# Layer 0's sums of squares as two float32r products (a high and a low part) instead of one fp32 product

## The chip, the core and the metric

The kernel runs on one core of a Trainium2 chip. The metric is the device time of one execution in microseconds (us), where lower is better. The core has a matrix engine (PE, with its weight loads listed apart as PEld), a vector engine (DVE), a scalar engine (ACT), a general engine (POOL) and a sync engine (SP) that here only issues DMAs. Each engine executes its own list of instructions in order and waits on semaphores for the others. SBUF is the on-chip memory, PSUM the accumulators that PE writes into and that DVE and ACT can read and write.

## The reference

The reference is a trunk of two layers on a sequence of 1024 positions and a width of 1024. Layer 0 mixes the tokens by differential attention, layer 1 by forgetting attention, and each is followed by a gated MLP with a short convolution. What the change touches is the norm behind the values of layer 0, over the 128 components of each of 8 heads:

```python
def rms_norm(x, g):
    xf = x.astype(jnp.float32)
    y = xf * lax.rsqrt(jnp.mean(xf * xf, -1, keepdims=True) + RMS_EPS) * g.astype(jnp.float32)
    return y.astype(x.dtype)
...
        s = jnp.einsum('bhcqd,bhckd->bhcqk', qb, k) * scale
        p = masked_softmax(s, causal_mask(start, Q_BLOCK, S))
        a = (p[:, :, 0] - lam * p[:, :, 1]).astype(v.dtype)
        o = jnp.einsum('bhqk,bhkd->bqhd', a, v)
        o = rms_norm(o, subln_g) * (1.0 - lambda_init)
```

and, in layer 1, the running sum of the forget gates, `c = jnp.cumsum(log_f, axis=1)`.

## The kernel before

**Products.** The inputs and the weights are fp32. A large product isn't done as one fp32 product but as three products in float32r, a shorter format that PE takes at a higher rate: `split` (lines 87 and 89) makes a high part by a copy on ACT and a low part by a subtraction on DVE, and `mm3` (lines 98 to 100) issues high by high, high by low and low by high into one accumulator. Nearly all lines of PE in the profile are therefore L98, L99 and L100.

**Layer 0's attention** takes about 60 to 540 us of the span. It runs over eight pairs of attention maps (one head of values each), some 57 us apiece. For each pair the loop in `attention` interleaves two streams by hand. One is the filler: 48 steps of `project`, the projection of the next pair's queries, keys and values (for the last pair: the output projection). The other is the pair's jobs. `diff_scores` makes one block of 128 queries against 128 to 1024 keys: PE products (L506, L507), a masked minimum on DVE (L509, into a small column `nm`), the exponential on ACT (L531), and normalising on DVE (L534 to L541). `Values` takes 256 queries at a time: it transposes the weights of the maps on PE by the identity (L1337), splits them into `pt` tiles (L87, L89), and multiplies them with the values (`m<-pt,q` at L98 to L100) into the left 256 columns of a PSUM bank, `ob`.

**The norm.** When such a value block is complete, `diff_values` runs, four times per pair and 32 times in all. In the layout here the 128 components of a head lie on the partitions, so the sum of squares runs over partitions. It copies the block out of PSUM (L553, ACT, `of<-m`), squares it (L556, ACT, into the left half of a 512-wide tile `sq`), and after two turns of the loop hands one fp32 product to a queue that the next turn empties: a matrix of ones by the squares (L562, PE, `m<-sq,ones`), 128x256, into the right half of the same bank `ob`. Every partition then holds the sum. ACT makes the reciprocal root by Ln and Exp (L567, L568, into the right half of `sq`) and its square (L569), and DVE multiplies (L571) and applies a correction step (L572, L573). The bank is free after L572.

**Buffers.** PSUM holds four banks of kind `m` (projections, transposes, values, norms) and two double banks of kind `s` (scores). The `wst` tiles, two of them, serve the staging of weights by DMA (L107) and also the second map's exponentials. Rotary steps move pieces of the projected tiles by DMA (L264, L454 to L469) and transpose them on PE (L475).

**Order.** The code above issues instructions in the order of the Python loop; the framework's scheduler then decides the order within each engine's list and the banks. A changed instruction can therefore move its neighbours too.

**Layer 1's gates.** `gate_logits` creates a constant tile `tri` and loads it (L592, L593). `forget_gates` forms the gates in a 1024-wide tile `w`, whose last 128 columns it leaves unused, and uses `ones` as an operand of a running sum. `forget_sums` multiplies by `tri` (L630).

Of the kernel before, what the change touches and what calls it, by code (L numbers as in the profile page):

```python
# [9 lines left out]
F32 = mybir.dt.float32  # L10
F32R = mybir.dt.float32r
BF16 = mybir.dt.bfloat16
I32 = mybir.dt.int32
AF = mybir.ActivationFunctionType
ALU = mybir.AluOpType
# [4 lines left out]
P = 128  # L20
# [34 lines left out]
class Trunk:  # L55
# [64 lines left out]
    def consts(self):  # L120
        nc, cp, i = self.nc, self.cp, self.i
        self.ident = cp.tile([P, P], F32, name="ident")
        nc.sync.dma_start(self.ident, i["ident"])
        mask = self.spare()[:, :P]
        nc.sync.dma_start(mask, i["mask"])

        self.mask = cp.tile([P, S], BF16, name="mask")
        nc.gpsimd.memset(self.mask[:, :S - P], 0.0)
        nc.vector.tensor_scalar(self.mask[:, S - P:], mask, -1.0, None, op0=ALU.mult)

        self.qz = [[cp.tile([P, P], F32R, name=f"qz{h}{b}") for b in range(2)] for h in range(2)]
        for h in range(2):
            for t in self.qz[h]:
                nc.gpsimd.memset(t[64 - 64 * h:128 - 64 * h, :].bitcast(F32), 0.0)
        self.nz = [0, 0]
        self.ones = cp.tile([P, P], F32, name="ones")
        nc.vector.memset(self.ones, 1.0)
        self.cw, self.cb = [], []
        for l in range(2):
            cw = cp.tile([P, NF, 3], F32, name=f"cw{l}")  # L140
            cb = cp.tile([P, NF], F32, name=f"cb{l}")
            nc.sync.dma_start(cw, i["cw"][l])
            nc.sync.dma_start(cb, i["cb"][l])
            self.cw.append(cw)
            self.cb.append(cb)
        self.eps_rms = cp.tile([P, 1], F32, name="eps_rms")
        nc.vector.memset(self.eps_rms, RMS_EPS)
        self.eps_ln = cp.tile([P, 1], F32, name="eps_ln")
        nc.vector.memset(self.eps_ln, LN_EPS)
        self.gsub = cp.tile([P, 1], F32, name="gsub")  # L150
        nc.sync.dma_start(self.gsub, i["subln"])
        nc.vector.tensor_scalar(self.gsub, self.gsub, (1.0 - LAM_INIT) * -0.5 / P, None, op0=ALU.mult)
# [397 lines left out]
    def diff_values(self, of, ob, c4):  # L550
        nc = self.nc
        osl = of[:, c4 * 256:c4 * 256 + 256]
        nc.scalar.copy(osl, ob[:, :256])  # L553
        sr = self.tp.tile([P, 512], F32, tag="sq", name=self.nm("sq"), bufs=1)
        sq, rd = sr[:, :256], sr[:, 256:]
        nc.scalar.activation(sq, osl, AF.Square)  # L556
        for _ in range(FL):
            yield

        ms, done = ob[:, 256:], []  # L560
        yield
        self.after(1, lambda: done.append(nc.tensor.matmul(ms, self.ones, sq, start=True, stop=True)))  # L562
        yield
        while not done:
            yield

        nc.scalar.activation(rd, ms, AF.Ln, scale=1.0 / P, bias=self.eps_rms)  # L567
        nc.scalar.activation(rd, rd, AF.Exp, scale=-0.5)  # L568
        nc.scalar.activation(sq, rd, AF.Square)  # L569
        yield  # L570
        nc.vector.scalar_tensor_tensor(osl, osl, self.gsub, rd, op0=ALU.mult, op1=ALU.mult)  # L571
        nc.vector.scalar_tensor_tensor(sq, ms, P * RMS_EPS, sq, op0=ALU.add, op1=ALU.mult)  # L572
        nc.vector.scalar_tensor_tensor(osl, sq, -3.0 * P, osl, op0=ALU.add, op1=ALU.mult)  # L573
# [4 lines left out]
    def gate_logits(self, c):  # L578
        nc = self.nc
        if c == 0:  # L580
            st = self.tmp()[:, :P]
            nc.sync.dma_start(st, self.i["wf"])
            w = self.tmp(F32R, pool=self.pp, tag="p")
            self.wf = w[:, :P], w[:, P:2 * P]
            for t in self.qz[0] + self.qz[1]:
                nc.gpsimd.memset(t[64:66, :].bitcast(F32), 1.0)
            self.split(*self.wf, st)
            self.bf = self.cp.tile([16, 1], F32, name="bf")
            nc.sync.dma_start(self.bf, self.i["bf"])
            self.z = self.tmp()  # L590
            self.zd = self.dr.tile([16, 1024], F32, name="zd")
            self.tri = self.cp.tile([P, P], F32, name="tri")  # L592
            nc.sync.dma_start(self.tri, self.i["tri"])  # L593
        ps = self.mbank()
        for kt in range(KT):
            ws = slice(16 * kt, 16 * kt + 16)
            self.mm3(ps[:16], self.wf[0][:, ws], self.wf[1][:, ws], self.xh[kt, c], self.xl[kt, c],
                     kt == 0, kt == KT - 1)
        nc.vector.tensor_scalar(self.z[:16, c * 512:c * 512 + 512], ps[:16], self.bf, None, op0=ALU.add)

    def forget_gates(self):

        nc = self.nc
        nc.sync.dma_start(self.zd, self.z[:16])
        w = self.tmp(pool=self.pp, tag="p")
        z, e, u, l, c = [w[:, j * P:j * P + P] for j in range(5)]
        self.chl = w[:, 5 * P:7 * P].bitcast(F32R)

        nc.sync.dma_start(z, self.zd.rearrange("h (b t) -> (h b) t", t=P))

        nc.vector.scalar_tensor_tensor(u, z, -1.0, z, op0=ALU.mult, op1=ALU.max)
        nc.scalar.activation(e, u, AF.Exp, scale=-1.0)
        nc.vector.tensor_scalar(u, e, 2.0, None, op0=ALU.add)
        nc.vector.reciprocal(u, u)
        nc.vector.tensor_tensor(e, e, u, op=ALU.mult)
        nc.vector.tensor_tensor(u, e, e, op=ALU.mult)
        nc.vector.tensor_scalar(l, u, 1.0 / 17, None, op0=ALU.mult)
        for k in (15, 13, 11, 9, 7, 5, 3, 1):
            nc.vector.scalar_tensor_tensor(l, l, 1.0 / k, u if k > 1 else e, op0=ALU.add, op1=ALU.mult)
        nc.vector.tensor_scalar(z, z, 0.0, None, op0=ALU.min)  # L620
        nc.vector.scalar_tensor_tensor(l, l, -2.0, z, op0=ALU.mult, op1=ALU.add)
        nc.vector.tensor_tensor_scan(c, self.ones, l, 0.0, op0=ALU.mult, op1=ALU.add)
        self.c = c

    def forget_sums(self, t):
# [924 lines left out]
```

## Time and profile before

| | |
|---|---|
| median of three runs | 2452.82 us (2452.7 to 2454.08) |
| span of the profiled execution | 2450.4 us |
| what lies around the span (median less span) | 2.4 us |
| PE / DVE / ACT busy, share of the span | 98% / 78% / 51% |
| share of the chain of waits: PE / DVE / DMA / ACT | 79% / 9% / 5% / 4% |

The page gives no second time for the profiled execution itself; its span and the 2.4 us around it stand for it. The profile was read on the span's own clock, with 0 at its first instruction. A row of the timeline begins with the start and the duration of one instruction; in square brackets stands the idle time of the engine ahead of it and what ended it. The durations of PE's instructions overlap, since the products are pipelined: what a product costs is the distance from its start to the next start, not its duration. On DVE and ACT too, one row's end can lie some 0.08 us behind the next one's start.

### The profile page before, as it was taken

Reading aid. Unit: us, or ns where it says so; the run is one execution under the profiler, and the core shown is the slowest. Engines: PE = TensorE matmul, PEld = TensorE weight load, DVE = VectorE, ACT = ScalarE, POOL = GpSimd, SP = SyncE. Lnnn points to the kernel's source line nnn. Section 1 sums busy time; section 2 is a strip of 40 time slices with the busy share of each in tenths; the row PEclk is TensorE's granted clock in tenths of the full one; section 3 lists DMA queues with packets and bytes.
Section 4 is the critical chain, followed back from the end, with each engine's and each line's share of the span. In section 5 each row is a group of like instructions: output and inputs, shape, how many; then the busy total and the mean of one; then the engine's idle time right before and its main releaser. Section 6 shows DMA issues by size and latency. Waiting matters only on the chain.

```text
span 2450.4 us, 33602 instructions
## 1 busy us (share of the span) xinstructions
PE 2411.6 (98%) x11803; PEld 2012.9 (82%) x11803; DVE 1908.4 (78%) x3731; ACT 1259.5 (51%) x2388; POOL 141.6 (6%) x321
## 2 busy tenths in 40 slices
PE   8999999999999999999999999999999999999998
PEld 6888888888888888888778888888888888888886
DVE  5777777989866677887867777778898676678977
ACT  4565666646544444544545555556465444445444
POOL 2101111110000000000101000000010000000000
PEclk9999999999999999999999999999999999999999
DMA  5232223622222223975232222224223222228751
GB/s 175 72 84 82 76 77 91 219 80 93 89 92 78 78 78 132 349 231 162 104 82 66 65 65 66 66 74 164 78 95 103 78 78 90 91 99 323 263 169 69
DMA packets 116033, 283.39 MB, mean 116 GB/s; under 512 B 18108, under 2 KB 25276, under 8 KB 115864
## 3 DMA queue, kind: packets, MB, share of 16 engines
q1 hardware_dynamic: 115064, 279.34, 35.5%
q8 instruction: 93, 1.52, 0.3%
q0 software_dynamic: 800, 1.90, 0.2%
q14 instruction: 76, 0.62, 0.1%
HBM read 188.44 MB, written 59.18 MB: 101 GB/s over the span
## 4 chain that ended last, share of the span: by engine, by line
PE 79%; DVE 9%; DMA 5%; ACT 4%; issue 2%; SPq 1%; POOL 0%; DVEq 0%; ACTq 0%; POOLq 0%
PE m L98 19%; PE m L100 19%; PE m L99 19%; PE s L98 3%; PE s L99 3%; PE s L100 3%; PE m L1337 3%; PE s L507 2%; PE s L506 2%; DMA wst<-in_w 1%; DMA pt<-in_wd 1%; PE m L1363 1%; PE m L1362 1%; DVE s L509 1%; DVE wo L89 1%
## 5 line engine op out<-in xcount | busy, mean ns | idle before, releaser
L98 PE MATMUL m<-xh,wh 128*128 128x512 f32 x768 | 322.8, 420 | 9.3 <-ACT xh L87 8.8
L100 PE MATMUL m<-xh,wl 128*128 128x512 f32 x768 | 304.3, 396 | 0.5 <-DVE wl L89 0.5
L99 PE MATMUL m<-xl,wh 128*128 128x512 f32 x768 | 302.1, 393 | 0.7 <-DVE xl L89 0.7
L98 PE MATMUL m<-xh,wo 128*128 128x512 f32 x656 | 255.5, 389 | 0.9 <-DVE xl L89 0.9
L99 PE MATMUL m<-xl,wo 128*128 128x512 f32 x656 | 255.2, 389 | 0.0
L100 PE MATMUL m<-xh,wo 128*128 128x512 f32 x656 | 255.2, 389 | 0.0
L509 DVE CUSTOM_DVE_ANT_0 s<-s,mask 128x128 f32<-128x128 f32 (+7 forms) x256 | 194.2, 759 | 48.2 <-PE s L507 47.5
L87 ACT ACTIVATE wo<-wg 128x512 fp32r<-128x512 f32 x168 | 106.2, 633 | 224.8 <-PE m L100 215.8
L87 ACT ACTIVATE pt<-m 128x512 fp32r<-128x512 f32 (+1 forms) x240 | 128.2, 552 | 127.6 <-PE m L1337 92.6
L98 PE MATMUL m<-q,wo 128*128 128x512 f32 x472 | 184.0, 390 | 0.0
L99 PE MATMUL m<-q,wo 128*128 128x512 f32 x472 | 183.6, 389 | 0.0
L100 PE MATMUL m<-q,wo 128*128 128x512 f32 x472 | 183.6, 389 | 0.0
L98 PEld LDWEIGHTS m<-xh,wh 128*128 128x128 f32 x768 | 145.7, 190 | 33.1 <-ACT xh L87 8.8
L100 PEld LDWEIGHTS m<-xh,wl 128*128 128x128 f32 x768 | 144.9, 189 | 33.1 <-DVE wl L89 1.5
L99 PEld LDWEIGHTS m<-xl,wh 128*128 128x128 f32 x768 | 146.0, 190 | 23.4 <-DVE xl L89 1.2
L89 DVE TENSOR_TENSOR pt<-m,pt 128x512 fp32r<-128x512 f32 (+1 forms) x240 | 148.6, 632 | 20.9 <-ACT pt L87 17.8
L87 ACT ACTIVATE wo<-t 128x512 fp32r<-128x512 f32 x132 | 82.8, 627 | 140.7 <-PE m L100 133.3
L501 POOL CAST qz<-q 64x128 fp32r<-64x128 f32 x256 | 97.7, 383 | 864.7 <-PE s L507 825.0
L89 DVE TENSOR_TENSOR wo<-wg,wo 128x512 fp32r<-128x512 f32 x168 | 115.2, 687 | 39.9 <-ACT wo L87 39.1
L98 PEld LDWEIGHTS m<-xh,wo 128*128 128x128 f32 x656 | 123.1, 188 | 27.2 <-PE m L929 1.4
L100 PEld LDWEIGHTS m<-xh,wo 128*128 128x128 f32 x656 | 123.2, 188 | 25.7
L99 PEld LDWEIGHTS m<-xl,wo 128*128 128x128 f32 x656 | 123.1, 188 | 25.3
(333 smaller groups left out, 6022.0 us busy)
## 6 DMA issues: line engine op xcount, KB each, us to landing
wst<-in_w SPq DMA_DIRECT2D x46, 512.0 KB
t<-in_wi SPq DMA_DIRECT2D x44, 512.0 KB
ha<-ad SPq DMA_DIRECT2D x88, 256.0 KB
wg<-in_wi SPq DMA_DIRECT2D x42, 512.0 KB
ad<-t SPq DMA_DIRECT2D x42, 512.0 KB
q<-q SPq DMA_DIRECT2D x128, 128.0 KB
pt<-in_wd SPq DMA_DIRECT2D x24, 512.0 KB
hb<-in_wd SPq DMA_DIRECT2D x44, 256.0 KB
```

The costliest lines, as they stand in the source:

```text
L87: nc.scalar.activation(hi, src, AF.Copy, scale=1.0 if scale is None else scale)
L89: nc.vector.tensor_tensor(lo, src, hi.bitcast(F32), op=ALU.subtract)
L98: mm(out, wh, xh, start=start, stop=False)
L99: mm(out, wh, xl, start=False, stop=False)
L100: mm(out, wl, xh, start=False, stop=stop)
L501: nc.gpsimd.tensor_copy(qz[r:r + 64, :], q[r:r + 64, qt * P:qt * P + P])
L506: nc.tensor.matmul(sb[:, ks], q[:, qt * P:qt * P + P], kd[:, ks], start=True, stop=False)
L507: nc.tensor.matmul(sb[:, ks], qz[rows], kl[rows, ks], start=False, stop=True)
L509: nc.vector.tensor_tensor_reduce(sb[:, :ln], sb[:, :ln], self.mask[:, S - ln:], 1.0, BIG, ALU.add, ALU.min, mn)
L1337: nc.tensor.transpose(tb[:, w:w + P], self.pts[q][:, kt * P:kt * P + P], k.ident)
L1362: mm(o, self.v[0][:, vs], h, start=first, stop=False)
L1363: mm(o, self.v[0][:, vs], l, start=False, stop=last)
```

## The change

The squares now go through PSUM and are split. ACT writes them into the right half of the bank (`ms`), copies them from there in float32r (`hi`), and DVE subtracts that from the squares (`lo`). PE then does two float32r products with a float32r matrix of ones, accumulated into `ms`, in place of the one fp32 product. The reciprocal root goes into the left half of the bank, its square into a new small tile `sr`. `tri` is no longer a tile of its own; it is loaded into the unused columns of `w` in `forget_gates`.

```diff
-        self.ones = cp.tile([P, P], F32, name="ones")
-        nc.vector.memset(self.ones, 1.0)
+        self.ones = cp.tile([P, P], F32R, name="ones")
+        nc.vector.memset(self.ones.bitcast(F32), 1.0)
...
         nc.scalar.copy(osl, ob[:, :256])
-        sr = self.tp.tile([P, 512], F32, tag="sq", name=self.nm("sq"), bufs=1)
-        sq, rd = sr[:, :256], sr[:, 256:]
-        nc.scalar.activation(sq, osl, AF.Square)
+        sr = self.tp.tile([P, 512], F32R, tag="sq", name=self.nm("sq"), bufs=1)
+        hi, lo = sr[:, :256], sr[:, 256:]
+        ms, done = ob[:, 256:], []
+        nc.scalar.activation(ms, osl, AF.Square)
+        nc.scalar.copy(hi, ms)
+        nc.vector.tensor_tensor(lo, ms, hi.bitcast(F32), op=ALU.subtract)
...
-        self.after(1, lambda: done.append(nc.tensor.matmul(ms, self.ones, sq, start=True, stop=True)))
+        def sums():
+            nc.tensor.matmul(ms, self.ones, hi, start=True, stop=False)
+            nc.tensor.matmul(ms, self.ones, lo, start=False, stop=True)
+            done.append(True)
+
+        self.after(1, sums)
...
+        sq, rd = self.tp.tile([P, 256], F32, tag="sr", name=self.nm("sr"), bufs=1), ob[:, :256]
...
-            self.tri = self.cp.tile([P, P], F32, name="tri")
-            nc.sync.dma_start(self.tri, self.i["tri"])
...
         self.chl = w[:, 5 * P:7 * P].bitcast(F32R)
+        self.tri = w[:, 7 * P:]
+        nc.sync.dma_start(self.tri, self.i["tri"])
...
-        nc.vector.tensor_tensor_scan(c, self.ones, l, 0.0, op0=ALU.mult, op1=ALU.add)
+        nc.vector.tensor_tensor_scan(c, self.ones.bitcast(F32), l, 0.0, op0=ALU.mult, op1=ALU.add)
```

In the changed program the lines of the norm are: Square L557, the copy to `hi` L558, the subtraction L559, the two products L566 and L567, then L576 to L578 on ACT and L580 to L582 on DVE (before: L567 to L569 and L571 to L573). The list of PE grows by 32 instructions, that of DVE by 32 instructions (30 rows, since some stand grouped), that of ACT by 32.

The order moves at many places. The first one shown is in pair 2, where the product follows soonest after its squares. PE's list there before (the names end in the number of the buffer; `m_1370` is the bank of the norm, `s_1523` a score bank):

```order
L100 MATMUL m_1507<-xh_250,wl_1140 128x512
L506 MATMUL s_1523<-q_564,q_562 128x512
L562 MATMUL m_1370<-sq_1385,ones 128x256
L507 MATMUL s_1523<-q_565,qz_300 128x512
L506 MATMUL s_1523<-q_564,q_562 128x256
L507 MATMUL s_1523<-q_565,qz_300 128x256
L98 MATMUL m_1531<-pt_1482,q_566 128x256
```

And PE's list now at the same place (`m_1384` is the bank of the norm, `s_1543` the scores, `m_1551` the values), from the fourth value product on; ahead of these rows stand the four score products and three value products:

```order
L98 MATMUL m_1551<-pt_1501,q_566 128x256
L99 MATMUL m_1551<-pt_1501,q_566 128x256
L100 MATMUL m_1551<-pt_1501,q_567 128x256
L98 MATMUL m_1527<-xh_256,wh_1147 128x512
L99 MATMUL m_1527<-xl_257,wh_1147 128x512
L100 MATMUL m_1527<-xh_256,wl_1148 128x512
L98 MATMUL m_1527<-xh_260,wh_1147 128x512
L566 MATMUL m_1384<-sq_1399,ones 128x256
L567 MATMUL m_1384<-sq_1399,ones 128x256
L99 MATMUL m_1527<-xl_261,wh_1147 128x512
```

The pair of products stands behind the four score products, six value products and four filler products, where the one product stood behind the first score product. DVE's list at the same place before:

```order
L534 RECIPROCAL rs_1587<-ls_1481 128x1
L536 TENSOR_SCALAR p_1545<-p_1545,rs_1587 128x768
L509 ISA s_1523,nm_1528<-s_1523,mask 128x768
L509 ISA nm_1528 128x1
L571 SCALAR_TENSOR_TENSOR of_1377<-of_1377,gsub,sq_1385 128x256
L572 SCALAR_TENSOR_TENSOR sq_1385<-m_1370,sq_1385 128x256
L573 SCALAR_TENSOR_TENSOR of_1377<-sq_1385,of_1377 128x256
L534 RECIPROCAL rs_1635<-ls_1530 128x1
```

And DVE's list there now:

```order
L534 RECIPROCAL rs_1607<-ls_1500 128x1
L536 TENSOR_SCALAR p_1565<-p_1565,rs_1607 128x768
L509 ISA s_1543,nm_1548<-s_1543,mask 128x768
L509 ISA nm_1548 128x1
L559 TENSOR_TENSOR sq_1399<-m_1384,sq_1399 128x256
L534 RECIPROCAL rs_1657<-ls_1550 128x1
L540 TENSOR_TENSOR rs_1657<-rs_1657,nlam 128x1
L541 SCALAR_TENSOR_TENSOR p_1565<-wst_1610,rs_1657,p_1565 128x768
L580 SCALAR_TENSOR_TENSOR of_1391<-of_1391,gsub,m_1384 128x256
L581 SCALAR_TENSOR_TENSOR sr_1517<-m_1384,sr_1517 128x256
```

The new subtraction (L559) stands right behind the minimum of the scores, and the norm's own last steps moved behind the normalising of the next map. The second place is on DVE in pair 3, ahead of the transposes of the rotary step. Before:

```order
L534 RECIPROCAL rs_2325<-ls_2235 128x1
L536 TENSOR_SCALAR p_2294<-p_2294,rs_2325 128x896
L89 TENSOR_TENSOR wl_2341<-wst_2256,wh_2340 128x1024
L509 ISA s_2282,nm_2287<-s_2282,mask 128x896
L509 ISA nm_2287 128x1
L89 TENSOR_TENSOR pt_2322<-m_2296,pt_2322 128x512
```

And now:

```order
L89 TENSOR_TENSOR wl_2380<-wst_2294,wh_2379 128x1024
L559 TENSOR_TENSOR sq_2284<-m_2222,sq_2284 128x256
L534 RECIPROCAL rs_2363<-ls_2271 128x1
L536 TENSOR_SCALAR p_2332<-p_2332,rs_2363 128x896
L509 ISA s_2320,nm_2325<-s_2320,mask 128x896
L509 ISA nm_2325 128x1
L89 TENSOR_TENSOR pt_2360<-m_2334,pt_2360 128x512
```

The low part of a weight slab (`wl`) moved ahead of the normalising of the first map (L534, L536), and the new subtraction stands between them. On SP, the load of that slab (L107, `wst_2256` before, `wst_2294` now) moved ahead of one DMA of the rotary step. SP's list in layer 1 takes the load of `tri` (L616) between the stores that end layer 0: five of them stand ahead of it, one and two weight loads behind it.

More of the change, by code (lines that the diff above doesn't have):

```diff
@@ L553, in diff_values @@
         nc.scalar.copy(osl, ob[:, :256])
-        sr = self.tp.tile([P, 512], F32, tag="sq", name=self.nm("sq"), bufs=1)
-        sq, rd = sr[:, :256], sr[:, 256:]
-        nc.scalar.activation(sq, osl, AF.Square)
+        sr = self.tp.tile([P, 512], F32R, tag="sq", name=self.nm("sq"), bufs=1)
[4 more added lines that the diff above has]
+        nc.vector.tensor_tensor(lo, ms, hi.bitcast(F32), op=ALU.subtract)
         for _ in range(FL):
             yield
-        ms, done = ob[:, 256:], []
         yield
-        self.after(1, lambda: done.append(nc.tensor.matmul(ms, self.ones, sq, start=True, stop=True)))
+        def sums():
[3 more added lines that the diff above has]
+        self.after(1, sums)
         yield
```

## Prediction

> **What bounds the kernel now.** I read the page's busy line and its chain of waits first, then busy time by windows of layer 0's attention, then the lines of the norm one by one.
>
> ```profile
> PE 2411.6 (98%) x11803; PEld 2012.9 (82%) x11803; DVE 1908.4 (78%) x3731; ACT 1259.5 (51%) x2388; POOL 141.6 (6%) x321
> PE 79%; DVE 9%; DMA 5%; ACT 4%; issue 2%; SPq 1%; POOL 0%; DVEq 0%; ACTq 0%; POOLq 0%
> 120.00:180.00 60.00, 59.61 (x321) 50.56 (x320) 47.26 (x113) 36.35 (x80) 5.48 (x17) 1.00 0.30 84
> 420.00:480.00 60.00, 57.77 (x310) 48.77 (x309) 54.84 (x127) 38.65 (x82) 7.95 (x15) 1.00 0.66 210
> 480.00:540.00 60.00, 59.40 (x302) 49.57 (x301) 52.28 (x105) 30.51 (x60) 3.73 (x8) 1.00 0.26 88
> sum 480.00, PE 468.30 PEld 397.37 DVE 390.10 ACT 287.89 POOL 53.07; mean PE 58.54 PEld 49.67 DVE 48.76 ACT 35.99 POOL 6.63
> ```
>
> The window rows give busy us of PE, PEld, DVE, ACT and POOL, then the granted clock of PE (1.00 in each); the sum is over the eight windows from 60 to 540. PE sets the end: it is busy for 98% and holds 79% of the chain. In the stretch that the change touches it stands still for only 0.4 to 2.2 us of each 60. DVE is the next one: 79% busy in the middle pairs (47.26 of 60), 91% and 87% in the last 120 us. So a microsecond of PE's own time is worth about a microsecond, if what feeds PE is ready earlier too, and added time on DVE is free in the middle and dear at the end. ACT has room everywhere.
>
> **What the norm's product costs PE.** The line's own view, two stretches of PE's timeline, and the place where the product waits:
>
> ```profile
> L562 PEld LDWEIGHTS m<-sq,ones x64: 186/188/192, 69.5 to 529.2; 128*128 128x128 f32 x64
> ...
>   ACT sq L556: 6.2, 13
> ```
>
> ```profile
> 90.24 0.39 PE L100 MATMUL m<-xh,wl 128*128 128x512 f32 x1
> 90.47 0.59 PE L562 MATMUL m<-sq,ones 128*128 128x256 f32 x2
> 90.71 0.59 PE L98 MATMUL m<-xh,wh 128*128 128x512 f32 x1
> 91.14 0.40 PE L99 MATMUL m<-xl,wh 128*128 128x512 f32 x1
> ...
> 133.58 0.28 PE L98 MATMUL m<-pt,q 128*128 128x256 f32 x1
> 133.70 0.28 PE L99 MATMUL m<-pt,q 128*128 128x256 f32 x1
> ```
>
> The 32 fp32 products appear as 64 records, two for each. From L100's start at 90.24 to L99's at 91.14 are 0.90 us, in which two 128x512 products of 0.23 (90.24 to 90.47) and the fp32 product run: 0.90 − 0.46 = **0.44 us** for it. A float32r product of the same 128x256 shape is 0.12 from start to start (133.58, 133.70), each with weights of its own; over longer rows of them (eight from 133.35 to 134.30 in that stretch) it is 0.117. The new pair is thus 0.235 us, and 0.44 − 0.235 = 0.205 us saved, 32 times: **−6.5 us**. This is the surest term. Its bounds: none saved, if float32r with `ones` were no cheaper (a rival below), and 6.5.
>
> **The wait ahead of it.** PE waits for the squares (L556) 13 times, records of PE and PEld together. Six products stand right behind their squares, the first of the four norms in each of pairs 2 to 7, at 132.58, 189.32, 247.13, 304.32, 362.32 and 419.31; the first and the last:
>
> ```profile
> 131.92 0.39 PE L506 MATMUL s<-q,q 128*128 128x512 f32 x1
> 132.58 0.70 PE L562 MATMUL m<-sq,ones 128*128 128x256 f32 x2 [0.27 <-ACT sq L556]
> 133.35 0.28 PE L506 MATMUL s<-q,q 128*128 128x256 f32 x1
> 133.47 0.28 PE L507 MATMUL s<-q,qz 128*128 128x256 f32 x1
> ...
> 419.31 0.70 PE L562 MATMUL m<-sq,ones 128*128 128x256 f32 x2 [0.27 <-ACT sq L556]
> ```
>
> From L506 to the next L506 are 1.43 us. Two 128x512 products and the fp32 one need 0.46 + 0.44 = 0.90, so 0.53 is lost at each, 3.2 in all. The other 26 products come late enough behind their squares that PE loses little there: the whole 6.2 us of that wait are mostly the same six counted on both PE and PEld.
>
> In the changed order the pair stands behind four score products, six value products and four filler products. PE reaches it at 131.92 + 2 × 0.23 + 8 × 0.117 + 4 × 0.23 = 134.24. Is `lo` ready then? On ACT and DVE stand:
>
> ```profile
> 132.10 0.42 ACT L556 ACTIVATE sq<-of 128x256 f32<-128x256 f32 x1
> ```
>
> ```profile
> 133.78 0.96 DVE L509 CUSTOM_DVE_ANT_0 s<-s,mask 128x768 f32<-128x768 f32 x1 [1.47 <-PE s L507]
> 134.67 0.14 DVE L509 DVE_READ_ACCUMULATOR2_ANT nm<- 128x1 f32 x1
> 134.67 0.48 DVE L571 SCALAR_TENSOR_TENSOR of<-of,gsub,sq 128x256 f32<-128x256 f32 x1
> ```
>
> The square ends at 132.5 there, and with the copy behind it `hi` is there at about 132.9; where the scheduler now puts one more 0.6 us evacuation ahead of it, at 133.5 at the latest. On DVE the subtraction comes behind the minimum (L509), which began 0.31 after the last score product had begun (133.47 to 133.78) and held DVE 0.89. That score product now begins at 131.92 + 0.46 + 0.117 = 132.50, the minimum at 132.81, the subtraction at 133.70, and it ends by 134.12, a tenth ahead of PE. So the wait goes, and the next thing late is nothing near: I take **−3.2 us**. The margin is a tenth; if the subtraction comes late the loss of 0.53 may stay, so the bounds are 0 and −3.2.
>
> **What is added on DVE and ACT.** No such copy or subtraction of 128x256 is in the trace; the nearest rows:
>
> ```profile
> L571 DVE SCALAR_TENSOR_TENSOR of<-of,gsub,sq 128x256 f32<-128x256 f32 x32 | 15.4, 481 | 2.5 <-ACT sq L568 2.0
> L572 DVE SCALAR_TENSOR_TENSOR sq<-m,sq 128x256 f32<-128x256 f32 x32 | 13.4, 419 | 0.7 <-ACT sq L569 0.7
> L553 ACT COPY of<-m 128x256 f32<-128x256 f32 x32 | 11.7, 367 | 23.9 <-PE m L100 23.9
> L89 DVE TENSOR_TENSOR pt<-m,pt 128x384 fp32r<-128x384 f32 x31 | 17.1, 553 | 1.8 <-ACT pt L87 1.1
> ```
>
> The copy out of PSUM is 0.37 us (L553), the subtraction 0.42 (L572, which reads PSUM and SBUF at the same size; the split of 128x384 at 0.553 bounds it from above). That is 32 × 0.37 = 11.8 us on ACT and 32 × 0.42 = 13.4 us on DVE. The other steps of the norm keep their number and size and only change between PSUM and SBUF; rows of either kind lie between 0.37 and 0.48, so I count them at 0, with ±0.07 each at most, on ACT and DVE where they are covered by idle time. On ACT the cover is 40% idle time. On DVE in pairs 1 to 6 it is 21% of idle time, some 12 us per pair against 4 × 0.42 = 1.7 us. Two places have no such cover.
>
> *The rotary transposes (L475).* Their wait is the largest of PE's in this stretch:
>
> ```profile
> PEld m L475 <- DVE pt L89: 8.5, 5, 2.2
> ```
>
> ```profile
> 203.49 1.15 DVE L541 SCALAR_TENSOR_TENSOR p<-wst,rs,p 128x896 f32<-128x896 f32 x1
> ...
> 209.95 1.22 DVE L89 TENSOR_TENSOR wl<-wst,wh 128x1024 fp32r<-128x1024 f32 x1 [1.03 <-ACT wh L87]
> ...
> 212.24 0.55 DVE L89 TENSOR_TENSOR pt<-m,pt 128x384 fp32r<-128x384 f32 x1
> ...
> 212.84 0.65 PE L475 MATMUL m<-ident,t 128*128 128x128 f32 x4 [1.57 <-DVE pt L89]
> ```
>
> In five pairs a chain ends here: L541 frees a `wst` tile, a weight slab is loaded into it, ACT and DVE split it (`wl` at 209.95), then minimum, `pt`, and the bank that L475 needs. One new subtraction now lies on DVE ahead of L541 in the same chain, behind the earlier `wl`. That is +0.42 per pair, 5 × 0.42 = 2.1 if nothing offsets it. The slab before it is loaded earlier now, ahead of a DMA of the rotary step; that can give back a part of the 1.03 us that DVE waited for `wh`. I take half of the added cost, **+1 us**, with bounds of −2.5 (half of the 1.03 gained in five pairs) and +5 (as much as that wait lost in five).
>
> *The last pair and the tail (420 to 540 us).* With DVE at 91% and 87%, PE's savings there are largely set by DVE. A quarter of the 32 products stands in these 120 of 480 us: 8 × 0.20 = 1.6 us of gain may not be collected, and 8 × 0.42 = 3.4 us are added to DVE. Bounds 0 and +5.0; I take **+2 us**, the lower half, because PE too was still 96 to 99% busy there (57.77 and 59.40 of 60).
>
> **The move of `tri`.** Before, its load stood early, and now it stands among the stores that end layer 0:
>
> ```profile
> L593 SPq DMA_DIRECT2D tri<-in_tri x1: 423/423/423, 51.0 to 51.0; - x1
> 1185.54 21.46 SPq L1482 DMA_DIRECT2D hd<-acc  x5
> ```
>
> SP spends 0.42 us on it. The stores around it take 21 us of SP's time while PE works on in layer 1, which hides it. I count 0; without that cover it would delay the weight loads behind it by 0.4, and longer only if it had to wait for its tile.
>
> **Sum.** −6.5 − 3.2 + 1 + 2 = −6.7 us. Against the profiled execution's span of 2450.4 and the 2.4 us around it, 2452.8, that is **2446 us**; the median of the runs shown is 2452.82, the same. The best ends (−6.5, −3.2, −2.5, 0) give 2440.6, the worst that keeps the saving (−6.5, 0, +5, +5) gives 2456.3.
>
> **Rivals.**
>
> *The gain is absorbed.* PE arrives 0.2 us earlier at every later wait, and if that wait is set by DVE (L475, banks freed by L89, the tail), it only gets longer. For it: DVE has got more work, not less, and 8.5 us of PEld's wait are at L475. Against it: in all of 60 to 540 us PE idles for 480 − 468.3 = 11.7 us, so DVE binds at few points. If only a quarter of the 9.7 remains, 2450.4. Chance 0.28.
>
> *The weights bind, and the pair is no cheaper.* The load of `ones` shows 188 ns, and the pair has two, 0.38 us, against 0.44: then 32 × 0.06 = 2 us are saved, 2450.8. Against it: the value products with a load each run at 0.12 in the rows above, so these loads lie beside the products. 0.07. The Trainium skill (Perfetto Trace Analysis, Identifying the Most-Contended Engine) says that PE's headroom is read from the busy share of the weight loads rather than from that of the products. The number of loads, 64, stays the same here, so by that rule alone nothing would be saved, 2452.8; the spacing of 0.12 at 188 ns a load speaks against it.
>
> *Slower: DVE is stopped in front of the minimum.* DVE runs in order. Where the subtraction stands ahead of a minimum (L509) and `hi` isn't there yet, DVE waits for square and copy, and 0.37 + 0.42 = 0.79 us pass before the minimum, the exponential behind it, and PE's next transposes and banks. If this reaches PE at 24 of 32 places, 24 × 0.79 = 19.0 us stand against 9.7: +9.3, 2462. It turns slower from 12 to 13 places. For it: PE waits on `pt` and on banks freed by DVE in the rows above. Against it: at both places shown the subtraction stands behind a minimum or a `wl`, when ACT has long copied. 0.10.
>
> **How the numbers follow.** Forecast 0.55, absorbed 0.28, weights 0.07, slower 0.10. The measurement of this kernel can tell about 0.2%, 4.9 us, from no change: faster means below 2447.9, slower above 2457.7. That gives 0.55 faster, 0.35 within, 0.10 slower. The range is 2440 to 2456: from the best ends of the terms to the worst, with the two middle rivals inside and the slower one left out.
>
> **What would show it.** Of the saving: L566 and L567 0.12 apart on PE, and PE's busy time in 60 to 540 us shorter by 6 us. Of the wait: no idle time at the six pairs, or one that now names DVE (`sq` at L559). Of DVE: 13.4 us more busy time, the subtraction at 0.42, without a new entry at L509. At L475 waits within half a microsecond of those before. It is wrong if a new wait of PE on DVE shows in most pairs, if the pair stands 0.4 apart, or if layer 1, where only `tri` changes, moves by over 1 us.

## The result, and the profile after

The changed kernel takes 2467.24 us in the median of five runs (2461.55 to 2471.29), against 2452.82 before: a ratio of 1.0059 with an interval of 1.0048 to 1.007. It is slower by 0.6%, beyond the range of the prediction. The profiled execution is the fastest of the five (2461.55 us, span 2459.8). The spread of 10 us is wide beside the 1.4 us of the five runs before, but in the later runs of this case the kernel before spread over 5.0 to 7.4 us too (21 to 28 runs each).

The page's busy line and chain of waits of the changed kernel:

```profile
PE 2410.2 (98%) x11803; PEld 2013.4 (82%) x11803; DVE 1919.4 (78%) x3763; ACT 1264.6 (51%) x2420; POOL 138.3 (6%) x321
PE 75%; DVE 10%; DMA 6%; ACT 4%; SPq 2%; issue 2%; DVEq 0%; POOL 0%; ACTq 0%
```

PE has lost four points of the chain, to DVE, DMA and SP's queue above all. Three windows of layer 0's attention (PE, PEld, DVE, ACT, POOL, then the granted clock), behind the first one as it was before:

```profile
180.00:240.00 60.00, 58.16 (x316) 49.60 (x315) 46.12 (x114) 37.11 (x82) 7.00 (x16) 1.00 0.28 76
...
180.00:240.00 60.00, 56.77 (x307) 48.59 (x307) 46.46 (x113) 36.18 (x82) 5.90 (x16) 0.97 0.27 76
300.00:360.00 60.00, 57.15 (x317) 48.92 (x316) 48.20 (x118) 37.20 (x84) 6.65 (x17) 1.00 0.28 76
420.00:480.00 60.00, 56.59 (x296) 47.58 (x296) 53.31 (x126) 38.27 (x85) 5.06 (x14) 0.97 0.66 211
```

And PE's wait at the rotary transposes from the view of waits, first as it was before, then the two lines of the changed kernel:

```profile
PE m L475 <- DVE pt L89: 6.3, 5, 1.8
...
PEld m L475 <- DVE pt L89: 16.4, 5, 3.6
PE m L475 <- DVE pt L89: 14.2, 5, 3.2
```

Two things stand there. PE's wait at L475, five times in pairs 3 to 7 as before, has grown from 6.3 to 14.2 us on PE. And the granted clock, 1.00 in every one of the eight windows before, is 0.97 in four of the eight now.

From the first score product to the first product of the MLP's weights, PE needed 519.5 us before (48.5 to 568.0) and 529.5 now (47.6 to 577.1). That is 10.0 us more, against 9.4 for the whole span: what lies ahead of this stretch and behind it is 0.6 us shorter. Within that stretch the pair itself does what it was meant to:

```profile
203.56 0.28 PE L566 MATMUL m<-sq,ones 128*128 128x256 f32 x1
203.68 0.28 PE L567 MATMUL m<-sq,ones 128*128 128x256 f32 x1
203.79 0.40 PE L98 MATMUL m<-xh,wh 128*128 128x512 f32 x1
```

The two products take 0.23 us in place of 0.44. In the groups by form, the added instructions cost what was estimated, and DVE hardly stops for the copy:

```profile
L559 DVE TENSOR_TENSOR sq<-m,sq 128x256 fp32r<-128x256 f32 x32 | 13.4, 419 | 0.5 <-ACT sq L558 0.5
L558 ACT CAST sq<-m 128x256 fp32r<-128x256 f32 x32 | 11.9, 371 | 0.8
L557 ACT ACTIVATE m<-of 128x256 f32<-128x256 f32 x32 | 12.4, 387 | 0.7
L577 ACT ACTIVATE m<-m 128x256 f32<-128x256 f32 x32 | 11.9, 372 | 0.5
```

Where does the wait at L475 come from? Here is the chain in pair 3, SP's queue first. Before (the first `wst` load, and the second, which is the one that L475 waits for in the end):

```profile
192.69 0.53 SPq L264 DMA_DIRECT2D q<-q  x1
193.26 0.58 SPq L107 DMA_DIRECT2D wst<-in_w  x1
193.94 1.55 SPq L264 DMA_DIRECT2D q<-t  x2
...
202.95 1.22 SPq L456 DMA_DIRECT2D t<-t  x2
204.27 1.33 SPq L107 DMA_DIRECT2D wst<-in_w  x1
```

And after, with DVE's and PE's rows of the same chain in a fence of their own behind them:

```profile
191.25 0.59 SPq L107 DMA_DIRECT2D wst<-in_w  x1
191.99 0.50 SPq L264 DMA_DIRECT2D q<-q  x1
...
193.89 0.53 SPq L264 DMA_DIRECT2D q<-q  x1
196.60 0.46 SPq L264 DMA_DIRECT2D q<-t  x1
...
203.55 1.84 SPq L456 DMA_DIRECT2D t<-t  x2
205.50 0.53 SPq L107 DMA_DIRECT2D wst<-in_w  x1
```

```profile
203.06 1.15 DVE L541 SCALAR_TENSOR_TENSOR p<-wst,rs,p 128x896 f32<-128x896 f32 x1
...
210.37 1.23 DVE L89 TENSOR_TENSOR wl<-wst,wh 128x1024 fp32r<-128x1024 f32 x1 [1.30 <-ACT wh L87]
...
213.26 1.11 PE L475 MATMUL m<-ident,t 128*128 128x128 f32 x4 [2.94 <-DVE pt L89]
```

Before, the first load (512 KB) was issued right behind the small move q<-q at 192.69. Now it is issued ahead of it. SP then stands from 194.4 to 196.6, and the view of SP's waits (188 to 210 us) says for what:

```profile
SPq L264 <- DMA q<-q: 2.1, 1, 2.1
```

It is the move q<-q that was issued at 191.99, some 4.6 us earlier. Before, a move that waited for the q<-q of 192.69 could go by 195.0, 2.3 us later. The semaphore events of the traces show the same in all of pairs 3 to 7: from its issue to its landing this move takes 4.5 to 4.9 us in the changed kernel, and 2.3 to 3.2 before. All rotary moves behind are late by that, and with them the second load. It is issued at 205.50 although L541 had freed its tile by 204.2; before, it was SP that stood ready at 204.27 and L541 that came last (204.6).

The same in the five pairs, each value taken from such rows (end of L541 to the end of the load's issue; start of L475 less the end of the product before it at 0.23 us):

| | pair 3 | pair 4 | pair 5 | pair 6 | pair 7 | sum |
|---|---|---|---|---|---|---|
| L541 to load issued, before | 0.96 | 0.30 | 0.16 | 0.66 | 0.31 | 2.4 |
| L541 to load issued, after | 1.81 | 1.43 | 1.05 | 2.35 | 0.05 | 6.7 |
| PE's loss at L475, before | 1.73 | 1.12 | 1.93 | 0.92 | 1.43 | 7.1 |
| PE's loss at L475, after | 3.10 | 3.38 | 2.95 | 3.34 | 2.28 | 15.1 |

In pair 7 the load is no longer late, and the loss still grows by 0.85 us, so the load's place is not all of it.

The lower clock lies right behind these losses. Two-microsecond windows around the first of them:

```profile
208.00:210.00 2.00, 2.00 (x11) 1.65 (x11) 1.04 (x3) 0.72 (x1) 0.00 (x0) 1.00 0.31 115
210.00:212.00 2.00, 0.32 (x2) 0.00 (x0) 1.63 (x2) 1.89 (x5) 0.00 (x0) 1.00 0.19 49
212.00:214.00 2.00, 0.73 (x4) 0.74 (x5) 2.00 (x6) 1.17 (x3) 0.00 (x0) 0.70 0.29 66
214.00:216.00 2.00, 2.00 (x7) 1.61 (x6) 1.79 (x5) 1.04 (x3) 0.00 (x0) 0.50 0.13 30
216.00:218.00 2.00, 2.00 (x14) 1.83 (x13) 1.28 (x5) 1.02 (x3) 0.29 (x1) 0.95 0.90 206
```

PE has nothing to do from about 210.3 to 213.3. The lost shares of the clock (0.30 + 0.50 + 0.05 of two us each, 1.7 us) are those of half clock for 3.4 us, from about 212.8 on. There are four such stretches, at 96, 212, 390 and 451 us (the first behind two waits of 1.4 and 1.1 us close together, the others behind L475), and none in the profile of before, apart from the last few us of the span, where both kernels are at half clock. PE's products in each take about 1.5 us longer than outside, 6 us together. Over the runs, the mean granted clock falls with the time (0.996 at 2461.55 and 2463.02 us, 0.995 at 2467.24, 0.993 and 0.994 at 2470.44 and 2471.29). One stretch takes 0.0007 off that mean (1.7 of some 2465 us), so the two slowest runs, at 0.002 and 0.003 less than the fastest, hold an estimated three to four stretches more. At about 1.5 us each that is some 4 to 6 of the 9 to 10 us between them; the rest of the spread isn't explained.

The account of the 10.0 us: −6.5 for the pairs, −3.2 for the six waits (none of PE's waits names the squares now), +7.9 at L475, +6 of half clock, and +3.3 of other waits of PE, nearly all on DVE (idle times above 0.1 us in PE's rows: 7.4 us, against 4.1 before, without L475 and L562). That is 7.5 in all. About 2.5 us are left, in waits too short for the view to list.

### The profile page after: what moved, and what is told of

Same layout as the page of the kernel before. It is cut to its first block, busy times and chain, and to the rows that moved or that the text cites. A ratio compares the mean times of both kernels' runs of the same rounds, so it can differ in the third digit from the quotient of the medians.

```text
span 2459.8 us, 33674 instructions
## 1 busy us (share of the span) xinstructions
PE 2410.2 (98%) x11803; PEld 2013.4 (82%) x11803; DVE 1919.4 (78%) x3763; ACT 1264.6 (51%) x2420; POOL 138.3 (6%) x321
## 4 chain that ended last, share of the span: by engine, by line
PE 75%; DVE 10%; DMA 6%; ACT 4%; SPq 2%; issue 2%; DVEq 0%; POOL 0%; ACTq 0%
PE m L98 19%; PE m L100 18%; PE m L99 18%; PE s L98 3%; PE s L100 3%; PE s L99 3%; PE m L1346 3%; DMA wst<-in_w 2%; PE s L507 2%; PE s L506 2%; PE m L1372 1%; DVE s L509 1%; PE m L1371 1%; DMA pt<-in_wd 1%; DVE wo L89 1%
## 5 line engine op out<-in xcount | busy, mean ns | idle before, releaser
L98 PE MATMUL m<-xh,wh 128*128 128x512 f32 x768 | 319.6, 416 | 10.3 <-ACT xh L87 9.5
```

What stands on the lines that cost most here:

```text
L98: mm(out, wh, xh, start=start, stop=False)
```

## The experiments

The theory after the result, **S**: the slab load's new place on SP makes L475 late, and the long waits lower the clock on top of that. The first rival, **D**: the added subtraction on DVE makes L475 late. Each kernel is compared with the kernel before as it was measured beside it: that median was 2449.66 or 2450.57 us here, where it had been 2452.82.

**The change with the loads held back, and the kernel before with the loads ahead.** A helper adds an issue order on SP, for the first load of each of pairs 3 to 7, and nothing else:

```diff
+LOADS = (186, 234, 282, 330, 378)
+LATE_LOADS = ((0, -6), (0, 3), (-5, 0))
+EARLY_LOADS = ((0, -7), (-6, 0), (2, 0))
+def pin(tc, edges):
...
+    for k in LOADS:
+        for later, earlier in edges:
+            tc.add_manual_dep(own[k + later], own[k + earlier].name,
...
+            if l == 0:
+                pin(self.tc, LATE_LOADS)
```

Here `own` is the list of SP's DMAs in the order of the code. The second kernel is the one before with `EARLY_LOADS`; its PE instructions keep their order.

> The change, with one thing held as before: in pairs 3 to 7 SP issues the weight slab's load (L107 of before) behind the first q<-q move and the four rotary moves that it stood behind before, and ahead of the next. Theory S (the load's place on SP made the transposes of L475 late: from the end of L541 to the load's issue 1.34 us on average in the changed kernel, 0.48 before): that distance falls to about 0.5 us, PE's waits at L475 fall from 15.0 us to 10 or 11, the half-clock stretches behind them become fewer, and the time falls to 2452 to 2458 us. Theory D (the added subtraction on DVE made them late): the waits stay at 14 to 15 us and the time at 2461 to 2471.

> The kernel before, with one thing taken from the change: in pairs 3 to 7 SP issues the weight slab's load ahead of the first q<-q move. Nothing on PE is changed. Theory S: the waits at L475 grow from 7.1 us to 11 or 12, and the time to 2456 to 2462 us (some half-clock stretches among it). Theory D: waits of 7 us and 2452 to 2454 us.

The change with the loads held back took 2452.34 us, 1.0005 of the kernel before (0.9996 to 1.0014): the whole slowdown is gone. The kernel before with the loads ahead took 2460.26, 1.0038 (1.0025 to 1.0052): most of the slowdown appears without any change on PE. PE's waits of the two kernels, the first with the loads behind:

```profile
PE m L491 <- DVE pt L105: 8.7, 5, 2.3
```

```profile
PE m L491 <- DVE pt L105: 10.1, 5, 2.6
```

(L491 is L475 of the other kernels; the helper moves the lines.) From the end of L541 to the load's issue are now −0.7 to 0.8 us with the loads behind, and 0.8 to 1.7 in the first four pairs with the loads ahead. By the measure of the table, PE's loss at L475 is 9.5 us with the loads behind and 10.9 with the loads ahead, each a little less than S had said. The move q<-q lands 2.3 to 2.5 us after its issue in the first kernel, as before, and 4.4 to 5.0 us in the second, as in the changed one. The first profile has no stretch of half clock, the second has two. S stands, from both sides, and so does the step in it that the move lands late behind the load. It doesn't account for all: the restored kernel should have been faster than before by the 9.7 us that PE saves, and is level.

**The high part alone, and the fp32 product with the added work.** The first leaves out the low part of the squares, so DVE gets nothing more; the second keeps the fp32 product and adds the copy and the subtraction. Both have the loads ahead.

```diff
-        nc.vector.tensor_tensor(lo, ms, hi.bitcast(F32), op=ALU.subtract)
...
-            nc.tensor.matmul(ms, self.ones, hi, start=True, stop=False)
-            nc.tensor.matmul(ms, self.ones, lo, start=False, stop=True)
+            nc.tensor.matmul(ms, self.ones, hi, start=True, stop=True)
```

```diff
+        nc.scalar.activation(s32, osl, AF.Square)
+        nc.scalar.copy(hi, s32)
+        nc.vector.tensor_tensor(spare, s32, hi.bitcast(F32), op=ALU.subtract)
...
+            nc.tensor.matmul(ms, self.ones.bitcast(F32), s32, start=True, stop=True)
```

> The change without the low part: no subtraction on DVE, and one float32r product (the squares rounded to float32r) where the change has two. SP issues the loads ahead of the q<-q moves, as in the change. PE does 32 x 0.117 = 3.7 us less than in the change, DVE 13.4 us less. Theory D: waits at L475 back at 7 to 8 us and a time of 2441 to 2447 us. Theory S: waits at L475 of 11 us or more, and 2452 to 2462 us.

> The kernel with the fp32 product, but with the change's copy on ACT and subtraction on DVE added (their results aren't used) and the change's other tiles. PE does what it did before, DVE 13.4 us more. SP issues the loads ahead of the first q<-q move, behind one of the moves. Theory D: waits at L475 of 10 to 13 us and 2456 to 2464 us. If DVE's added work is free and only the load's place counts: waits of 9 to 12 us by the load alone, and the distance from the end of L541 to the load's issue above 0.9 us; if that distance is at 0.5 and the waits still grow, it is DVE.

The high part alone took 2451.33 us, level with before (1.0, 0.9992 to 1.0009), and PE's waits at L475 were 11.8 us: S was right about the waits there, and the time lies 0.7 us below its range. The fp32 product with the split took 2464.68, 1.0056 (1.0043 to 1.0068), with 12.6 us at L475, three stretches of half clock, and 1.6 us from L541 to the load in three of five pairs. It is 4.4 us above the kernel with the loads ahead and nothing added. So D may have a part too, a smaller one; this kernel has one stretch of half clock more than that one, and its squares lie in SBUF.

**The same with the loads held back, and the subtraction moved or doubled.** Two new names for what absorbs PE's saving once the loads are back: **D2**, the added subtraction; **A**, PE only arrives earlier at waits that DVE sets. The four kernels: the low part made on POOL from squares in SBUF (the diff), the high part alone, the fp32 product with the split, and the change with the subtraction written twice; all four with `LATE_LOADS`.

```diff
+        nc.scalar.activation(sq, osl, AF.Square)
+        nc.scalar.copy(hi, sq)
+        nc.gpsimd.tensor_tensor(lo, sq, hi.bitcast(F32), op=ALU.subtract)
```

> The change with the loads held behind the q<-q move as before, and with the low part made on POOL (from squares that ACT leaves in SBUF) in place of DVE. PE does the same as in the change. Theory D2 (with the loads back in their place, the added subtraction on DVE, ahead of L541, is what absorbs PE's saving of 9.7 us): waits at L475 of 6 to 8 us, and 5 to 9 us faster than the kernel before on the same chip. Theory A (PE only arrives earlier at waits that DVE sets anyway, whatever is added): within 2 us of the kernel before.

> One float32r product of the high part, no subtraction, the loads behind the q<-q move as before. PE does 32 x (0.44 - 0.117) = 10.3 us less than before and has no wait of 3.2 us for a product at once behind its squares if it is moved as in the change. Theory D2: 8 to 13 us faster than the kernel before, waits at L475 of 6 to 8 us. Theory A: 1 to 5 us faster, waits at L475 of 10 us or more. Against the same kernel with the loads ahead (2451.3): theory S says 4 us or more faster.

> The fp32 product kept, copy and subtraction added (results unused), the loads behind the q<-q move as before: only ACT's and DVE's added work is left of the change. Theory D2: 5 to 9 us slower than the kernel before, waits at L475 above 9 us. Theory A: within 2 us of it. Against the same kernel with the loads ahead (14.1 us above the kernel before on that chip): theory S says at least 6 us less.

> The change with the loads behind the q<-q move as before, and the subtraction done twice: DVE gets another 13.4 us of work. Theory D2: 4 to 9 us slower than the same kernel with one subtraction (which was 1.8 us above the kernel before), waits at L475 2 us or more above its 9.5. Theory A: within 2 us of it.

| kernel, loads held back | median us (before 2449.66) | ratio, interval | PE's wait at L475 |
|---|---|---|---|
| low part on POOL | 2447.04 | 0.999 (0.9982 to 0.9999) | 1.8 |
| high part alone | 2445.71 | 0.998 (0.9971 to 0.9989) | 7.7 |
| fp32 product with split | 2457.05 | 1.003 (1.0018 to 1.0042) | 8.9 |
| subtraction twice | 2453.06 | 1.0012 (1.0003 to 1.0021) | 8.4 |

S holds again in size, taking each kernel against the one before that was measured beside it: the high part alone is 3.9 us faster than before with the loads back, where it was 0.8 slower, and the fp32 product with the split loses 7.4 where it lost 14.1. Between D2 and A the runs are divided. The doubled subtraction adds 32 rows of 0.42 us on DVE (8.2 us of busy time, 1918.8 to 1927.0) and some 1.6 us to the time (3.4 above before, where one subtraction was 1.8 above), which is A's; two stretches of half clock are in its profile, and none in that of one subtraction. The split on an fp32 product costs 7.4, which is D2's; but there DVE stopped for ACT's copy:

```profile
DVE sr L576 <- ACT sq L575: 3.9, 8, 0.6
```

That is 3.9 us, against 0.5 in the change, and one stretch of half clock is in its profile, so its price is not that of the work alone. And the low part on POOL took L475's wait almost away, from 8.7 to 1.8 us. It was 2.6 us faster than before, so 4.4 us better than the same with the subtraction on DVE (1.8 above before). That lies between the theories, D2 with 5 us or more faster than before and A within 2. The products now waited for POOL:

```profile
PE m L584 <- POOL sq L576: 2.3, 8, 0.6
PE m L491 <- DVE pt L105: 1.8, 4, 0.6
```

**Nothing added at all, the tile alone, POOL with more time, and the change again.** In the first, ACT writes the squares in float32r and one product sums them (the low part is left out); the loads are held back. The second is the kernel before with only `tri` moved. The third is the kernel with POOL and one more `yield` ahead of the products.

```diff
+        nc.scalar.activation(hi, osl, AF.Square)
...
+            nc.tensor.matmul(ms, self.ones, hi, start=True, stop=True)
```

```diff
-        for _ in range(FL):
+        for _ in range(FL + 1):
```

> ACT writes the squares rounded to float32r, and one float32r product sums them: no copy, no subtraction, nothing added on DVE or ACT (the low part is left out). The loads stand behind the q<-q move as before. PE does 32 x (0.44 - 0.117) = 10.3 us less than before. Theory A (what PE saves is mostly waited for again at DVE's later points, whatever is added): 2 to 6 us faster than the kernel before. Theory D2 (the added copy and subtraction took the gain): 9 to 13 us faster.

> The kernel before with only the load of tri moved into layer 1, to the unused columns of w. If the move is free, as forecast: within 1 us of the kernel before, and waits at L475 of 7 us in layer 0 as before. If the move holds the weight loads behind it: over 2 us slower.

> The low part on POOL, the loads behind the q<-q move, and the pair of products one turn of the loop later. In the run without the later turn PE waited 2.3 us for POOL's low part and 1.1 us for ACT's high part. If those waits are worth their time: gone, and 1 to 3 us faster than that run (which was 2.6 us faster than the kernel before), so 3.5 to 5.5 us faster than before. Theory A (PE only waits elsewhere): within 1 us of that run.

> The change as it is, on the chip of the other runs of this call. 8 to 18 us slower than the kernel before, with three to nine stretches of half clock, each behind a wait of PE at L475 or at a bank freed by DVE.

With nothing added the kernel took 2443.78 us against 2450.57, 0.9971 (0.9959 to 0.9982): 6.8 us faster, of 10.3 that PE no longer does. That lies between the two theories. PE waits 9.5 us at L475 there, 3 more than before. So about a third of what PE saves is waited for again, though DVE and ACT do no more than before. `tri` alone: 2450.13, 0.9998 (0.9989 to 1.0006), no difference. POOL with one more turn: 2446.47, 0.9981 (0.9972 to 0.999), 4.1 us faster than before; the waits that it was to remove are still there (2.0 us for POOL, 1.1 for ACT), so its mechanism was wrong, and its gain over the kernel without the turn lies within the intervals. Of the kernels that keep both parts of the squares it is the fastest, and faster than both kernels of this case. The change again: 2462.59 us against 2450.57, 1.0054 (1.0041 to 1.0067), with four stretches of half clock, two of them nearly 7 us long.

## Why the prediction was wrong

- **What a product costs: right.** 0.23 us for the pair in place of 0.44, −6.5 us. The rival that the weight loads bind is out: each of the pair's two loads still shows 188 ns.
- **The wait for the squares: right.** None of PE's waits is left there; the weight loads wait 1.1 us in six places for the subtraction, at most 0.2 at a time.
- **The added instructions: right.** 0.419 and 0.371 us against 0.42 and 0.37. DVE's busy time grew by 11.0 us, not by the 13.4 of the sum, which fits neighbouring rows that overlap by some 0.08 us each.
- **The rotary transposes: this step failed.** "The slab before it is loaded earlier now, ahead of a DMA of the rotary step; that can give back a part of the 1.03 us that DVE waited for `wh`." The moved load was seen and given the wrong sign. It was counted for itself and not for what stands behind it in SP's queue: a small move whose landing the next rotary moves wait for. They, and the second load behind them, became late. The term was +1 us with bounds of −2.5 and +5; it measured +7.9. The loads held back take 5.6 of that away (15.1 to 9.5 by the table's measure). The prediction's own sign, waits at L475 within half a microsecond of those before, failed in each of the five pairs (+0.85 to +2.42).
- **A consequence that was no term: the clock.** With waits of up to 3.4 us at L475, the granted clock halves behind some of them. That is 6 us in the profiled run, and by the estimate above a part of the spread of the others.
- **The last pair and the tail: too dear, as far as the last pair goes.** From the seventh pair's store (477.9 before, 487.7 after) to the MLP (568.0 and 577.1) the changed kernel is 0.7 us faster; +2 had been taken.
- **`tri`: right**, no difference by itself.
- **The rivals.** "The gain is absorbed" is what remains when the loads are held back: level with before. The runs show a part of its mechanism: with nothing added, a third of PE's saving is waited for again. The rival on the other side, DVE stopped in front of the minimum, did not happen (DVE waited 0.5 us in all for the copy); the kernel became slower by a way that stood on no list.

What stays open is how the 9.7 us divide, in the change with the loads held back, between the subtraction and PE's earlier arrival. A second subtraction costs 1.6 us, and taking the first one off DVE, to POOL, brings 4.4. That is less than half of the 11.5 us between the forecast gain of 9.7 and the 1.8 that was lost; the kernel with nothing added shows that 3.5 of 10.3 go without any subtraction. The intervals are some 2 us wide on either side, and each kernel is also ordered anew by the scheduler.

## What to carry to other kernels

When a change shifts the order on a queue that issues DMAs, follow what stands behind the shifted transfer, not the transfer alone: here a large load issued ahead of a small move doubled the time until that move landed, and all that waited for it became late. An engine that is busy 98% of the time can still owe its time to a chain through a queue and a shared buffer; what it saves ahead of such a chain's end is partly waited for there. And a wait of two or three microseconds on PE can cost 1.5 us more behind it, through the clock, depending on when it falls.

## What the hardware showed

**The clock.** Stretches of half clock followed waits of PE of 2.1 us (the kernel with `tri` alone, at 270 us) to 3.7 us (the change again, at 212); after waits of 3.4 and 3.0 us in the changed kernel's profile (pairs 4 and 5), and of 1.9 us and less before, there was none. What decides is where the wait falls. In each profile the clock records put every halving on a grid with steps of 3.413 us; in the changed kernel the later three stand 34, 86 and 104 steps behind the first. Over the fourteen profiles, half clock followed each of the 31 steps in which PE was busy for at most 1.45 us (14 of these end the span), and of the others, apart from two that were at half clock already, only one of 1.64. The step from 209.37 to 212.78 us had 0.95 us of work. The wait of 3.4 us in pair 4 fell into two steps with 2.13 and 1.48 us of work, and the clock stayed. This is read from the records; no run moved a wait to test it. The Trainium skill (TensorE: Matmul & The Clock Gate, What's actually happening) has the clock halve after an idle window of about 3.4 us that runs freely against the program. The length of the window agrees; but the window need not be idle throughout, and a wait well under 3.4 us was enough here.

**ACT and PSUM.** The norm's ACT steps got faster when their operands moved into PSUM: the exponential, with both operands moved, took 372 ns where it was 415, and the first square, with its output moved, 387 where it was 414. The logarithm and the second square, with one operand moved each, gained 29 and 33 ns. The Trainium skill (Perfetto Trace Analysis, Optimizing Scalar/DVE Operations) states some 93 ns of access overhead on SBUF and 51 on PSUM for this engine; the difference of 42 is close to the 43 that the exponential gained. The page adds in brackets that these are engine-busy times and that the profiled latency is about twice this; a gain of twice 42 does not show in these profiled durations.
